# Attention with the two heads of a pair worked off side by side, in a two-layer hybrid encoder on one core

## The chip, the cores and the metric

The kernel runs on 1 core of one Trainium2 chip. The metric is the device time of one execution in microseconds (us); less is better. TensorE (PE; its weight loads stand apart as PEld), VectorE (DVE), ScalarE (ACT), GpSimd (POOL) and the DMA queues work side by side and wait for each other by semaphores.

## The reference, cut to what matters

One sequence of 512 tokens with 1024 features goes through two layers. Each layer has a mixer (a state-space part S5, six heads of latent attention MLA, six heads of forget-gate attention FOX, normalised, merged and projected back) and a feed-forward part: dense in the first layer, eight experts with two per token in the second. The attention that the change touches is a softmax over the keys up to the end of the queries' block of 128:

```
def block_sweep(q, k, v, scale, mask_fn, log_decay=None):
    for qb in range(L // Q_BLOCK):                 # 4 blocks of 128 queries
        q0, q1 = qb * Q_BLOCK, (qb + 1) * Q_BLOCK
        s = q[:, :, q0:q1] @ k[:, :, :q1]^T * scale
        if log_decay is not None:
            s = s + log_decay[:, :, q0:q1, None] - log_decay[:, :, None, :q1]
        s = where(mask, s, -inf)
        p = softmax(s)
        outs.append(p @ v[:, :, :q1])
    return concatenate(outs, axis=2)
```

A head is 64 wide in v. All of it is float32.

## The kernel before

Program order is written in Python; which instruction stands where in an engine's own queue is laid down before the run by a planner (`tile.TileContext(nc, schedule_with_timeline_sim=True)`), which plays the program through and takes, on each engine, the earliest in program order of what is ready. A tile's buffer is taken when its first writer is placed, and comes free with its last reader. On the chip each engine then works strictly through its queue.

**Layers.** `layer_mix` walks the strings of `SEQ` (L104, L105): a letter is a step, among them `f` and `m` (project and lay out a pair of heads of FOX or MLA), `s` and `o` (S5), `a` (adaLN vectors, each piece a DMA of 512 KB into one buffer and a product on DVE, L473 to L482; held behind the last pair of heads laid out, L471), `A` (attention of the next pair that was laid out), `g` (merge one mixer's output), `w` (one eighth of the output projection). There are six pairs of heads in a layer, three of FOX and three of MLA, so six `A` steps.

**A pair of heads.** `attend` (L893) goes through head 0's four query tiles and then head 1's, eight tiles in all. For tile i with n = i + 1 key blocks:

- `att_prob` (L860): the logits into a bank of PSUM group A (two banks; L867, and the mask at L868), the maximum on DVE (L871), the exponential with its sum on ACT into a tile `pr` of 128 x 512 (L872; `NPR` = 3 buffers), the reciprocal (L873) and the scaling by it (L874: on GpSimd for i = 0 and 2, on DVE for i = 1 and 3).
- `att_out` (L877), traced two tiles later (`ADP` = 2): n transposes of `pr` into a bank of PSUM group B (three banks; L883), one copy to the tile `PT` on ACT (L886; two buffers), and n products with v (L888), each 64 output rows wide. Head 0 puts out to rows 0 to 63 of the pair's bank `po`, head 1 to rows 64 to 127; `po` is one more bank of group B. A float32 product is two instructions on the PE queue.
- after the last tile `po` is copied to the pair's place in the mixer's output (L891).

**The output projection** `out` (L1235) borrows the buffers of `pr` for a tile `xs` of x: loaded by a DMA on ACT's queue (L1237), updated on DVE from PSUM (L1244), and stored by another DMA on ACT's queue (L1245). After the mixer x is loaded again from there (L1264) and the MLA part of the projection is added (L1272, L1273).

Of the kernel before, what the change touches and what calls it, by code (L numbers as in the profile page):

```python
# [10 lines left out]
FT = mybir.dt.float32  # L11
# [38 lines left out]
# places of all experts, and of all but the last two  # L50
# [3 lines left out]
def _most_blocks():  # L54
    """The most blocks of 128 tokens that can be left over, for any counts of the experts."""
# [3 lines left out]
    while todo:  # L59
        r, top, used, k = todo.pop()  # L60
        best = max(best, k)
        if r == NE or (r, top, used, k) in seen:
            continue
        seen.add((r, top, used, k))
        # the smallest counts at which rank r leaves j blocks, and the same count as the rank before
        for n in {min(top, CAP[r])} | {CAP[r] + P * j + 1 for j in range(NT)} | {top}:
            if n <= top and used + n <= 2 * L:
                todo.append((r + 1, n, used + n, k + max(0, -(-(n - CAP[r]) // P))))
# [14 lines left out]
NPR = 3  # L83
# [114 lines left out]
def lay(inputs):  # L198
# [11 lines left out]
    # the scales of the first norm with their inputs on partitions  # L210
# [76 lines left out]
class Net:  # L287
    def __init__(self, ctx, tc, a, out, dbg=None, depth=DEPTH, stop=None):
# [10 lines left out]
        # what needs other activation tables  # L299
# [18 lines left out]
    def consts(self):  # L318
# [11 lines left out]
        for l in range(DEPTH):  # L330
# [8 lines left out]
            # the gains of q and k meet in the products: k carries both  # L339
# [16 lines left out]
    def bank(self, side=None):  # L356
        """A bank of PSUM: of the group asked for, or of each in turn."""
# [9 lines left out]
    def wload(self, src, n, eng=None, pool=None, tag="", bufs=2):  # L367
        """A piece of a weight as two parts that the tensor engine takes in one pass each."""
# [18 lines left out]
    def exp_ln(self):  # L387
        """The activation tables with both Exp and Ln, for what is traced in the block this opens."""
# [8 lines left out]
    def mm3(self, ps, a, b, start, stop, shared=False):  # L397
        """Three passes; shared: the bank holds two groups, and the first start clears it for both."""
# [5 lines left out]
    def rsqrt_of(self, ps, n, m, out, tmp):  # L404
        """1 / sqrt(ps / n + EPS)"""
# [13 lines left out]
    def sigmoid(self, x, scale):  # L419
        """x = 1 / (1 + exp(-scale x)), the exponential kept finite."""  # L420
# [41 lines left out]
    def ada_prep(self):  # L462
        """silu(c), with its features on partitions and along the free dimension."""
# [5 lines left out]
    def held(self):  # L469
        """What VectorE gets in the block stays behind the last pair of heads laid out."""  # L470
# [16 lines left out]
    def norm_sum(self, x, groups):  # L487
        """The sum of squares of each token, on all partitions; the squares of a group are added up beforehand."""
# [12 lines left out]
    def norm_rms(self, ps, cut=1):  # L501
        """1 / the root mean square of each token, on all partitions, in parts that can be had one by one."""
# [9 lines left out]
    def norm_block(self, x, k, r, A, sh, h, s=slice(0, L)):  # L512
        """A block of features, normalised and modulated, in two parts."""
# [22 lines left out]
    def start(self, x, h, names, ps):  # L536
        """The first norm block by block, as the weights of its modulation come in, and what the blocks give to the
        first projections."""
# [57 lines left out]
    def angles(self, pool):  # L596
        """Sines and cosines of the positions and of what S5 turns by, in a step and in a chunk of 8; its decays."""
# [31 lines left out]
    def powers(self, t, tmp, last):  # L629
        """t[i, :, k] = t[i, :, 0] ** (k + 1), complex."""  # L630
# [8 lines left out]
    def s5_mats(self, l, q0, nq, pool):  # L639
        """The matrices of nq pairs of groups: inputs to states, states to outputs, inputs to outputs in a chunk."""  # L640
# [32 lines left out]
        # (lam_bar - 1) / lam  # L673
# [26 lines left out]
        # -Im(H) and Re(H): the conjugate of C and of the powers gives Re(H) and -Im(H)  # L700
# [13 lines left out]
        # the two groups of a pair side by side, each on its own half of the rows  # L714
# [25 lines left out]
        # the rotation of chunk j by 8 j times the angle, and the decay of a chunk  # L740
# [11 lines left out]
    def s5_part(self, l, u, c, yj, pool):  # L752
        """A quarter of the groups: the chunks' states by a scan, and what the groups put out."""
# [72 lines left out]
    def s5_out(self, l, yj, pool):  # L826
        """The gated output, features on partitions."""
# [15 lines left out]
        # gelu(y) = y sigmoid(2 sqrt(2 / pi) (y + 0.044715 y^3))  # L843
# [16 lines left out]
    def att_prob(self, un, hh, i, pool):  # L860
        """The softmax of a head for a tile of queries."""
# [8 lines left out]
        pr = pool.tile([P, L], FT, tag="pr", name="pr", bufs=NPR)  # L870
# [6 lines left out]
    def att_out(self, un, hh, i, pr, po, pool, oT):  # L877
        """Its product with v, by keys on partitions."""
        nc = self.nc
        ps = self.bank("B")  # L880
        n = (i + 1) * P
        for j in range(i + 1):
            nc.tensor.transpose(ps[:, j * P:(j + 1) * P], pr[:, j * P:(j + 1) * P], self.C("ident"))  # L883
        PT = pool.tile([P, L], FT, tag="PT", name="PT", bufs=NPT)
        eng = nc.scalar.copy if (hh * NT + i) % 8 in PTA else nc.vector.tensor_copy
        eng(PT[:, :n], ps[:, :n])  # L886
        for j in range(i + 1):
            nc.tensor.matmul(po[hh * 64:hh * 64 + 64, i * P:n], un["v"][:, j, un["vo"] + hh, :],  # L888
                             PT[:, j * P:(j + 1) * P], start=(j == 0), stop=(j == i))
        if hh == 1 and i == NT - 1:  # L890
            nc.scalar.copy(oT[:, un["u"], :], po)  # L891

    def attend(self, un, pool, oT):  # L893
        """A pair of heads: the softmax of a tile runs ahead of the product of the one before."""
        po = None
        for hh in range(2):
            for i in range(NT):
                pr = self.att_prob(un, hh, i, pool)
                self.att_end(ADP)
                if po is None:  # L900
                    po = self.bank("B")
# [1007 lines left out]
```

## Time and profile before

| | us |
|---|---|
| median of 3 runs | 1623.21 |
| lowest, highest of the 3 | 1614.22, 1625.42 |
| span of the profiled execution, first to last instruction | 1614.5 |

The profiled execution is thus like the fastest of the three runs. In the order of time the span holds the start and the first layer's mixer (to about 345 us), the dense feed-forward part (to about 740 us), the second layer's mixer (to about 1004 us) and the experts. Matmuls are pipelined and a matmul's length in the profile covers its way through the array, so the distance from start to start is what one costs in a row of them. Queue waits are inferred from semaphores.

### The profile page before, as it was taken

The page shows a single profiled execution, that of the slowest core. Times are in us where ns is not written, and L with a number is a line of the kernel's source. Part 1 is how long each engine was busy: PE and PEld are TensorE (multiplying, and loading weights), DVE is VectorE, ACT ScalarE, POOL GpSimd, SP SyncE. Part 2 cuts the span into 40 slices and gives each one's busy share as a digit, 9 for nine tenths or more (in the row PEclk, how much of TensorE's full clock was granted, in tenths as well). Part 3 has the DMA queues.
Part 4 walks back from the last instruction along what each step waited for, and adds up shares of the span by engine and source line. Part 5 has one row for each costly group of instructions (what it writes and reads, how often), then busy time and mean ns, then how long its engine had stood idle before and what let it go on. Part 6 is the DMA issues. An engine that isn't in the chain of part 4 may idle for free.

```text
span 1614.5 us, 25527 instructions
## 1 busy us (share of the span) xinstructions
PE 1524.0 (94%) x8907; PEld 1288.6 (80%) x8907; DVE 1129.4 (70%) x2628; ACT 805.2 (50%) x1547; POOL 200.7 (12%) x279
## 2 busy tenths in 40 slices
PE   6989999889999999999999999599999999999997
PEld 5877776568888788888877667489889999998995
DVE  7695677775855577556455565778678878877876
ACT  4344357443322232234345763366566766766762
POOL 1223131111000000003221120100000001003002
PEclk7988899989999999999999999789999999999998
DMA  9323341575566657553321006377688878878886
GB/s 358 132 91 124 118 134 46 189 274 158 182 200 187 228 168 233 174 169 115 115 78 48 1 8 221 114 247 270 233 275 298 281 236 309 304 260 297 305 281 212
DMA packets 94823, 309.62 MB, mean 192 GB/s; under 512 B 12065, under 2 KB 12513, under 8 KB 94689
## 3 DMA queue, kind: packets, MB, share of 16 engines
q1 hardware_dynamic: 74736, 252.89, 47.0%
q0 software_dynamic: 13040, 42.45, 7.7%
q10 hardware_dynamic: 6912, 12.59, 2.3%
q8 instruction: 72, 1.18, 0.3%
q14 instruction: 63, 0.51, 0.1%
HBM read 283.79 MB, written 24.10 MB: 191 GB/s over the span
## 4 chain that ended last, share of the span: by engine, by line
PE 66%; DMA 14%; DVE 11%; issue 4%; ACT 3%; POOL 1%; SPq 0%; DVEq 0%; ACTq 0%; POOLq 0%
DMA adw<-in_wada_dram 6%; PE psB L401 4%; PE psB L400 4%; PE psB L402 4%; PE psC L401 3%; PE psC L400 3%; PE psC L402 3%; PE psB L888 3%; PE psA L402 3%; PE psA L400 3%; PE psA L401 3%; PE psA L867 3%; PE psB L1427 2%; PE psA L1427 2%; DVE adw L478 2%
## 5 line engine op out<-in xcount | busy, mean ns | idle before, releaser
L383 ACT CAST wh<-wr 128x1024 fp32r<-128x1024 f32 (+4 forms) x402 | 396.8, 993 | 424.5 <-PE psB L401 90.4
L384 DVE TENSOR_TENSOR wl<-wr,wh 128x1024 fp32r<-128x1024 f32 (+4 forms) x402 | 459.1, 1149 | 162.8 <-ACT wh L383 158.2
L478 DVE SCALAR_TENSOR_TENSOR adw<-adw,cact 128x1024 f32<-128x1024 f32 x80 | 98.1, 1227 | 75.5 <-DMA adw<-in_wada_dram 75.4
L1427 PE MATMUL psB<-hgB,wh 128*128 128x480 f32 (+3 forms) x256 | 85.3, 341 | 0.0
L867 PE MATMUL psA<-U 65*128 65x128 f32 (+3 forms) x192 | 72.2, 463 | 8.3 <-DVE xn L981 7.6
L871 DVE TENSOR_REDUCE ms<-psA 128x1 f32<-128x128 f32 (+1 forms) x96 | 46.4, 485 | 45.6 <-PE psA L868 45.1
L1429 PE MATMUL psB<-hgB,wl 128*128 128x256 f32 x256 | 72.2, 282 | 0.0
L1427 PE MATMUL psC<-hgB,wh 128*128 128x480 f32 (+3 forms) x192 | 65.9, 348 | 0.2 <-ACT wh L383 0.2
L874 POOL TENSOR_SCALAR pr<-pr,ms 128x128 f32<-128x128 f32 (+1 forms) x48 | 49.0, 1021 | 136.5 <-DVE ms L873 100.2
L400 PE MATMUL psB<-fh,wh 128*128 128x512 f32 (+1 forms) x156 | 61.2, 392 | 4.7 <-ACT fh L518 4.7
L1427 PE MATMUL psA<-hgB,wh 128*128 128x480 f32 (+3 forms) x184 | 63.1, 350 | 1.0 <-ACT wh L383 0.7
L401 PE MATMUL psB<-fh,wh 128*128 128x512 f32 (+1 forms) x156 | 60.9, 390 | 0.3 <-DVE fh L523 0.3
L402 PE MATMUL psB<-fh,wl 128*128 128x512 f32 (+1 forms) x156 | 60.6, 388 | 0.0
L872 ACT ACTIVATE pr<-psA,ms 128x128 f32<-128x128 f32 (+1 forms) x96 | 51.4, 537 | 18.0 <-DVE ms L871 13.2
L1507 POOL DMA_DIRECT2D yd<-yt x21 | 11.8, 563 | 375.9 <-ACT yt L1497 263.1
L886 ACT COPY PT<-psB 128x128 f32<-128x128 f32 (+1 forms) x96 | 41.5, 435 | 31.5 <-PE psB L883 31.2
L1429 PE MATMUL psA<-hgB,wl 128*128 128x256 f32 x184 | 53.3, 290 | 3.0 <-DVE wl L384 3.0
L1429 PE MATMUL psC<-hgB,wl 128*128 128x256 f32 x192 | 55.2, 287 | 0.0
L1427 PEld LDWEIGHTS psB<-hgB,wh 128*128 128x128 f32 x256 | 48.4, 189 | 1.6
L1429 PEld LDWEIGHTS psB<-hgB,wl 128*128 128x128 f32 x256 | 48.4, 189 | 0.2
L867 PEld LDWEIGHTS psA<-U 65*128 65x128 f32 (+1 forms) x192 | 32.4, 204 | 14.9 <-issue 11.1
L883 PE MATMUL psB<-cst,pr 128*128 128x128 f32 x240 | 44.2, 290 | 0.0
(772 smaller groups left out, 4608.4 us busy)
## 6 DMA issues: line engine op xcount, KB each, us to landing
adw<-in_wada_dram SPq DMA_DIRECT2D x80, 512.0 KB, 3.8
wr<-in_md_dram SPq DMA_DIRECT2D x80, 512.0 KB, 4.5
wr<-in_mg_dram SPq DMA_DIRECT2D x79, 512.0 KB, 4.7
wr<-in_mu_dram SPq DMA_DIRECT2D x78, 512.0 KB, 4.7
wr<-in_fg_dram SPq DMA_DIRECT2D x22, 512.0 KB, 4.4
wr<-in_fu_dram SPq DMA_DIRECT2D x22, 512.0 KB, 4.4
wr<-in_me_dram SPq DMA_DIRECT2D x16, 512.0 KB, 4.3
wr<-in_w_f_dram SPq DMA_DIRECT2D x12, 512.0 KB, 3.7
```

The costliest lines, as they stand in the source:

```text
L383: nc.scalar.copy(hi[:, :n], raw[:, :n])
L384: nc.vector.tensor_tensor(out=lo[:, :n], in0=raw[:, :n], in1=hi[:, :n], op=OP.subtract)
L400: mm(ps, a[0], b[0], start=start, stop=False, skip_group_check=shared)
L401: mm(ps, a[0], b[1], start=False, stop=False, skip_group_check=shared)
L402: mm(ps, a[1], b[0], start=False, stop=stop, skip_group_check=shared)
L478: nc.vector.scalar_tensor_tensor(out=w, in0=w, scalar=1.0, in1=self.cact, op0=OP.mult, op1=OP.mult, accum_out=self.ada[l][:, j:j + 1])
L867: nc.tensor.matmul(ps[:, :n], U[0:r, 2 + hh, i * P:n], U[0:r, hh, 0:n], start=True, stop=False)
L872: nc.scalar.activation(pr[:, :n], ps[:, :n], AF.Exp, bias=ms[:, 0:1], accum_out=ms[:, 1:2])
L874: (nc.gpsimd if (hh * NT + i) % 8 in PRP else v).tensor_scalar(pr[:, :n], pr[:, :n], ms[:, 1:2], None, op0=OP.mult)
L888: nc.tensor.matmul(po[hh * 64:hh * 64 + 64, i * P:n], un["v"][:, j, un["vo"] + hh, :], PT[:, j * P:(j + 1) * P], start=(j == 0), stop=(j = ...
L1427: mm(ps[:, :2 * C], hi[:, s], h2, start=(kk == 0), stop=False, skip_group_check=True)
L1429: mm(ps[:, C:C + 2 * P], lo[:, s], h2[:, 0:2 * P], start=False, stop=(kk == KD - 1), skip_group_check=True)
```

## The change

All comments and docstrings are dropped, which moves line numbers and nothing else. What is computed stays the same.

- `attend` goes through the four tiles and takes both heads of a tile together; `att_out` gets both heads' probabilities, transposes and copies one head after the other, and then runs the products key block by key block, head 0 and head 1 in turn.
- What was traced two tiles later is now traced two pairs of tiles later.
- `pr` becomes two tiles by the parity of i, `pr0` of 384 columns and `pr1` of 512, with two buffers each in place of three of 512.
- `out` takes its `xs` from `pr1`, and so has two buffers in place of three.

```diff
-NPR = 3
+NPR = 2
 NPT = 2
@@ att_prob
-        pr = pool.tile([P, L], FT, tag="pr", name="pr", bufs=NPR)
+        pr = pool.tile([P, L - P + P * (i % 2)], FT, tag=f"pr{i % 2}", name="pr", bufs=NPR)
@@
-    def att_out(self, un, hh, i, pr, po, pool, oT):
-        """Its product with v, by keys on partitions."""
+    def att_out(self, un, i, prs, po, pool, oT):
         nc = self.nc
-        ps = self.bank("B")
         n = (i + 1) * P
+        PTs = []
+        for hh, pr in enumerate(prs):
+            ps = self.bank("B")
+            for j in range(i + 1):
+                nc.tensor.transpose(ps[:, j * P:(j + 1) * P], pr[:, j * P:(j + 1) * P], self.C("ident"))
+            PT = pool.tile([P, L], FT, tag="PT", name="PT", bufs=NPT)
+            eng = nc.scalar.copy if (hh * NT + i) % 8 in PTA else nc.vector.tensor_copy
+            eng(PT[:, :n], ps[:, :n])
+            PTs.append(PT)
         for j in range(i + 1):
-            nc.tensor.transpose(ps[:, j * P:(j + 1) * P], pr[:, j * P:(j + 1) * P], self.C("ident"))
-        PT = pool.tile([P, L], FT, tag="PT", name="PT", bufs=NPT)
-        eng = nc.scalar.copy if (hh * NT + i) % 8 in PTA else nc.vector.tensor_copy
-        eng(PT[:, :n], ps[:, :n])
-        for j in range(i + 1):
-            nc.tensor.matmul(po[hh * 64:hh * 64 + 64, i * P:n], un["v"][:, j, un["vo"] + hh, :],
-                             PT[:, j * P:(j + 1) * P], start=(j == 0), stop=(j == i))
-        if hh == 1 and i == NT - 1:
+            for hh, PT in enumerate(PTs):
+                nc.tensor.matmul(po[hh * 64:hh * 64 + 64, i * P:n], un["v"][:, j, un["vo"] + hh, :],
+                                 PT[:, j * P:(j + 1) * P], start=(j == 0), stop=(j == i))
+        if i == NT - 1:
             nc.scalar.copy(oT[:, un["u"], :], po)
 
     def attend(self, un, pool, oT):
         po = None
-        for hh in range(2):
-            for i in range(NT):
-                pr = self.att_prob(un, hh, i, pool)
-                self.att_end(ADP)
-                if po is None:
-                    po = self.bank("B")
-                self.pend.append(lambda hh=hh, i=i, pr=pr, po=po: self.att_out(un, hh, i, pr, po, pool, oT))
+        for i in range(NT):
+            prs = [self.att_prob(un, hh, i, pool) for hh in range(2)]
+            self.att_end(ADP)
+            if po is None:
+                po = self.bank("B")
+            self.pend.append(lambda i=i, prs=prs, po=po: self.att_out(un, i, prs, po, pool, oT))
@@ out
-                    xt = pool.tile([P, L], FT, tag="pr", name="xs", bufs=NPR)
+                    xt = pool.tile([P, L], FT, tag="pr1", name="xs", bufs=NPR)
```

## Rows read from the trace of the kernel before

**Rows 1.** The page, part 1: busy us, share of the span, instructions.

```profile
PE 1524.0 (94%) x8907; PEld 1288.6 (80%) x8907; DVE 1129.4 (70%) x2628; ACT 805.2 (50%) x1547; POOL 200.7 (12%) x279
```

**Rows 2.** Stretches: length, busy PE, PEld, DVE, ACT, POOL, then clock, DMA, GB/s.

```profile
100.00:262.00 162.00, 155.41 (x971) 119.02 (x970) 109.78 (x428) 81.69 (x233) 45.13 (x69) 0.91 0.34 108
262.00:345.00 83.00, 76.79 (x345) 53.45 (x344) 66.25 (x123) 46.40 (x92) 7.88 (x9) 0.98 0.61 211
831.00:982.00 151.00, 148.38 (x916) 106.26 (x915) 93.26 (x295) 97.23 (x256) 30.57 (x45) 1.00 0.12 37
```

**Rows 3.** Waits of PE in 831 to 982 us: total us, times, longest.

```profile
PE psB L888 <- ACT PT L886: 1.2, 3, 0.5
```

**Rows 4.** Timeline of PE at 216 us: start, length, line, tile, form, count.

```profile
215.77 0.50 PE L883 MATMUL psB<-cst,pr 128*128 128x128 f32 x3
216.19 0.65 PE L888 MATMUL psB<-PT,vm 128*64 128x128 f32 x4
216.77 0.66 PE L883 MATMUL psB<-cst,pr 128*128 128x128 f32 x4
217.27 0.60 PE L960 MATMUL psC<-cst,xn 128*65 128x128 f32 x4
217.70 0.60 PE L867 MATMUL psA<-U 65*128 65x256 f32 x2
```

**Rows 5.** Timeline of PE at 205 us, S5 and attention next to each other.

```profile
205.26 0.32 PE L822 MATMUL psD<-sB,sU 128*64 128x128 f32 x1
205.27 0.32 PE L888 MATMUL psB<-PT,vm 128*64 128x128 f32 x1
205.42 0.27 PE L822 MATMUL psD<-sB,sU 128*64 128x128 f32 x1
205.43 0.27 PE L888 MATMUL psB<-PT,vm 128*64 128x128 f32 x1
```

**Rows 6.** Timeline of PE at 858 us: S5's products, halves in turn.

```profile
858.14 0.69 PE L786 MATMUL psD<-sU,sC 128*64 128x64 f32 x16
858.66 0.60 PE L888 MATMUL psB<-PT,vf 128*64 128x128 f32 x4
```

**Rows 7.** Instructions of lines 888 and 886: ns min, median, max, first and last start.

```profile
L888 PE MATMUL psB<-PT,vf x240: 272/273/477, 121.0 to 934.5; 128*64 128x128 f32 x120
...
L886 ACT COPY PT<-psB x96: 252/460/672, 106.3 to 969.5; 128x128 f32<-128x128 f32 x24, 128x256 f32<-128x256 f32 x24, 128x384 f32<-128x384 f32 x24, 128x512 f32<-128x512 f32 x24
...
  PEld psB L888: 9.4, 17
```

**Rows 8.** Timelines of ACT and PE around two tiles' products at 950 us.

```profile
946.78 0.48 ACT L886 COPY PT<-psB 128x384 f32<-128x384 f32 x1
947.95 0.58 ACT L886 COPY PT<-psB 128x512 f32<-128x512 f32 x1 [0.22 <-PE psB L883]
...
950.21 0.87 PE L888 MATMUL psB<-PT,vm 128*64 128x128 f32 x6
```

**Rows 9.** Line 874, the scaling on GpSimd: ns min, median, max.

```profile
L874 POOL TENSOR_SCALAR pr<-pr,ms x48: 594/1233/2137, 103.1 to 962.4; 128x128 f32<-128x128 f32 x24, 128x384 f32<-128x384 f32 x24
```

**Rows 10.** Landing of the xs loads (L1237), then of the xs stores (L1245).

```profile
DMA to landing us min/median/max: 2.6/4.9/7.8
...
DMA to landing us min/median/max: 2.0/4.6/9.0
```

**Rows 11.** Line 1244 in 970 to 1004 us, six of its eight.

```profile
L1244 DVE SCALAR_TENSOR_TENSOR xs<-psC,ada,xs x6: 740/748/751, 976.4 to 1002.2; 128x512 f32<-128x512 f32 x6
```

**Rows 12.** The chain that ended last, 989 to 1003 us: start, us, what.

```profile
989.72 6.29 DMA xs<-xs
...
996.09 6.05 DMA xs<-xd
...
1003.02 0.38 PE psC L1537
```

**Rows 13.** The adaLN pieces of the first mixer: the chain, then line 478.

```profile
294.05 5.96 DMA adw<-in_wada_dram
...
L478 DVE SCALAR_TENSOR_TENSOR adw<-adw,cact x15: 1212/1224/1573, 226.5 to 349.3; 128x1024 f32<-128x1024 f32 x15
```

## The prediction

> **What bounds the kernel now.** I read the page first, for who is busy over the span: the tensor engine 94% of it [rows 1]. That share is an average, so next came the table by stretches. In the second layer's attention, 831 to 982 us, PE is busy 148.4 of 151.0 us while DVE has 93 and ACT 97: PE is the bound there [rows 2]. In the first layer, 100 to 262 us, it is 155.4 of 162.0, nearly the same but with more holes. From 262 to 345 us it is 76.8 of 83.0 [rows 2], and there the chain of waits runs through adaLN pieces: a load of up to 6.0 us into the one buffer, 1.2 us of DVE, the next load [rows 13]. So work taken from PE shortens the second layer's attention nearly one to one, the first layer's in part, and what stands behind its adaLN chain hardly at all. Then I read the timelines of PE, for what a product with v costs in its surroundings, and the views of the xs tiles, because the change takes one of their buffers.
>
> **The products side by side.** A pair of heads has 2 x (1+2+3+4) = 20 products of two instructions, 40; twelve pairs make the 480 of line 888, in two rows of 240 of which one is shown [rows 7]. In a row each costs what any 128-column float32 instruction does: the four of L960 take 217.70 - 217.27 = 0.43 us, 0.108 each [rows 4]. What two of them cost on different halves of the output rows the trace of before shows by chance: S5's last product and head 0's first stand next to each other, start 0.01 us apart, and so do their second instructions [rows 5]. That two halves in turn keep this up inside one bank is seen at S5's input products: sixteen 64-column instructions in 858.66 - 858.14 = 0.52 us, 0.033 each, where half of 0.108 would be 0.054 [rows 6]; that interval holds a change of form too. The queue takes instructions in order and each half can run one at a time. With a1 a2 b1 b2 a1 a2 ... the second of one head runs beside the first of the other, so 4n instructions of a pair of tiles need 2n + 1 places in time instead of 4n. Over n = 1 to 4 that is 24 places for 40: 16 saved, 16 x 0.108 = 1.73 us a pair, 10.4 us a layer.
>
> **The changes of form.** Between instructions with 64 and with 128 columns of the array PE loses time. Three transposes before a burst of products take 0.42 us to its start (0.095 over 3 x 0.108), the four products 0.58 us (0.15 over), the four transposes behind them 0.50 us (0.07 over) [rows 4]: 0.31 us a burst. There are at most 96 bursts, one for each copy to PT [rows 7]; both heads in one burst leave 48. That is 24 x 0.31 = 7.4 us a layer. The Trainium skill says the same in TensorEngine Tiling (Array Packing), Key Properties: changing the tiling mode drains the engine. It gives no price; the 0.31 us above is the trace's.
>
> **How much of it comes.** All of it is 17.8 us a layer, if both PT are there when PE reaches the products. None of it comes if the planner places head 0's products as soon as its PT is ready, while head 1's copy (0.25 to 0.67 us) still runs [rows 7]: head 0's block of at most eight instructions, 0.87 us, would be mostly gone by then. In before PE mostly comes late: a weight load of L888 waited for a PT only 17 times for 96 copies [rows 7], in the second layer PE waited 3 times, 1.2 us in all [rows 3], and at 950 us the next tile's PT had been finished (947.95 + 0.58) before the products of the tile ahead began [rows 8]. So about 80 of 100 are ready. The planner sees its own times and not the chip's, so I take 0.7: 12.4 us of PE time a layer.
>
> **The softmax in pairs.** Instructions, engines and sizes stay the same. New is that the exponential of tile i + 2 needs the buffer of tile i of the same parity, so it waits for the transposes of tile i; and for i = 0 and 2 both heads' scalings go to GpSimd one behind the other, 2 x 1.23 us [rows 9]. That loop (exponential, scaling twice, transposes 0.43 a head, copies) is some 5 us for two tiles' worth of both heads, against 151 / 6 / 2 = 12.6 us of PE work for them, so it is covered by the projections and logits that PE does meanwhile. Without that cover, in the last pair, it shows: 2 to 4 us a layer. Below it can cost nothing, above all of one GpSimd pair exposed twice in each pair of heads, 6 x 2 x 1.23 = 15 us a layer. It is nearer to the lower end, since PE waits so little today; I take 3 us in the second layer and 2 us in the first. The second bank of group B that both heads' transposes want is there (three banks, one for `po`), so at nothing; if a projection holds it, it is one copy late, 0.5 us.
>
> **The xs tiles.** Each of eight steps loads (median 4.9 us), updates (0.75), stores (4.6) [rows 10, 11], 10.3 us around one buffer and about 10.8 with issue. With three buffers the eighth step needs two rounds behind the first, with two it needs three: 32 us. The steps of the second layer spread over about 26 us today, up to 1002.2 [rows 11], and their end already waits: store 6.3 us, load 6.1 us, and only then PE's next [rows 12]. Behind the waiting update stand the release of its bank of group C and what DVE has queued; behind the store's wait on ACT's queue stand the casts of the next weights. So the last update comes 6 us later than it could. Least: nothing (three rounds at the shortest landings, 2.6 + 2.0 + 0.75, are 16 us). Most: at 7.8 and 9.0 us, 53 us against 26. PE has the MLA part of the projection to do meanwhile, so I take 4 us in the second layer and, with the slower transfers of 262 to 345 us but a longer spread, 3 us in the first.
>
> **The sum.** Second layer: -12.4 + 3 + 4 = -5.4 us. First layer: five of its six pairs lie ahead of 268 us, -10.3 us on PE; with holes and S5's loads on the path I count six tenths, -6; +2 and +3 behind: about -1 (what shortens the last pair goes into the wait for adaLN, which ends at 349.3 + 1.2 us [rows 13] and moves with the start of its pieces). Other stages do the same work. Together about -6.5 us: 1614.5 - 6.5 = 1608 us against the profiled execution. That one is like the fastest of three runs; the median, 1623.2, stands 8.7 us above it. Taken from the median: 1617 us.
>
> **Rivals.**
>
> *All of it comes, the tails stay hidden.* 17.8 us in the second layer and most of it, 11 to 15, in the first: 1623 - 30 = 1593 us. For it: PE busy 98% in the second layer [rows 2], and the two places where halves run together [rows 5, 6]. Against it: the planner, two buffers for xs.
>
> *The products don't run side by side.* A rule of the Trainium skill speaks for this: TensorE: Matmul & The Clock Gate, Part 3, "What overlaps and what doesn't", says that a weight load overlaps running matmuls only when the row group differs, and here both heads use all 128 rows. The trace disagrees: both products at 205 us hold 128 rows and still start together [rows 5], and the sixteen at 858 us too are on 128 rows [rows 6]. As a mechanism here, without overlap: only the changes of form are saved, 0.7 x 7.4 = 5.2 us a layer, less the new waits of 12 us: 1623 - 10 + 12 = 1625 us. The same time comes when the planner undoes the alternation.
>
> *Two xs buffers become the bound at both mixers' ends: slower.* At three rounds of 6.3 + 6.1 + 0.75 + 0.5 = 13.7 us [rows 12] the eight steps take 41 us against 26: +15 us in the second layer, about +10 in the first, where DMA is busy 0.61 [rows 2]; with 12 us gained on the way, 1623 + 25 - 12 = 1636 us. It decides when a round is over 1.5 times what PE needs for two steps. For it: that chain is on the path today. Against it: the first layer's spread is long already, and PE has other work.
>
> **How the numbers follow.** About 1% is what a measurement of this kernel can tell from no change, some 16 us; the three runs alone spread over 11. Forecast (1608 to 1624) 0.42; all of it (1588 to 1607) 0.27; no overlap or no alternation (1620 to 1632) 0.16; the xs bound (1630 to 1650) 0.15. Faster by over 1% is below 1607: the second case and a little of the first and third, whose ends reach there with the noise, 0.32. Slower by over 1% is above 1639: most of the last and a little for a planner that lays out queues worse elsewhere, 0.16. Within 1% is left with 0.52. The range leaves out the better end of the second and the worse end of the last: 1592 to 1637; the forecast's own is 1608 to 1624.
>
> **What would show it.** Right: products of the two heads starting in twos less than 0.02 us apart, in about 48 bursts; the second mixer's attention some 10 us shorter with PE still over 95% busy; the last update of xs 4 to 6 us later behind the last product with v than today. Wrong on the overlap: twos that start 0.108 us apart. Wrong on the alternation: runs of one head's products ahead of the other's. Wrong on the softmax: PE waits for `pr` or PT of more than 3 us a layer. Wrong on xs: eight updates within 26 us, or over 35. What would upset all of it is a change in length of the feed-forward or expert stages, of which no row here tells.

## The result and the profile after

The changed kernel takes 1637.8 us (median of four runs, 1633.4 to 1639.7) against 1622.0 us of the kernel before (four runs on the same chip, 1614.2 to 1625.4): ratio 1.0103, with a 95% interval of 1.008 to 1.0126. It is slower by about 1%, and it lies just outside the range forecast, 1592 to 1637 us (the forecast itself was 1617). The span of the profiled execution grew from 1614.5 to 1636.8 us.

The page's first part, as in [rows 1]: the engines did the same work, with PE busy 3.4 us less, in a longer span.

```profile
PE 1520.6 (93%) x8907; PEld 1278.6 (78%) x8907; DVE 1128.8 (69%) x2628; ACT 806.4 (49%) x1547; POOL 199.4 (12%) x279
```

The table by stretches (length, busy PE, PEld, DVE, ACT, POOL, granted clock, DMA share, GB/s). The first three lines answer [rows 2]; the second layer's attention starts 12 us later here, so its stretch is 843 to 994 us. The other three are stretches at the lower clock, which are read further down.

```profile
100.00:262.00 162.00, 155.92 (x1013) 116.70 (x1011) 113.02 (x437) 88.19 (x246) 45.95 (x70) 0.92 0.33 107
262.00:345.00 83.00, 69.78 (x297) 47.85 (x294) 61.76 (x112) 39.25 (x76) 5.71 (x8) 0.92 0.62 209
843.00:994.00 151.00, 143.29 (x904) 99.24 (x903) 92.15 (x291) 96.67 (x253) 28.33 (x44) 0.97 0.11 33
...
892.00:903.00 11.00, 10.07 (x40) 6.66 (x40) 3.21 (x14) 2.36 (x7) 1.63 (x6) 0.53 0.09 28
1022.00:1036.00 14.00, 12.08 (x35) 9.51 (x36) 7.18 (x12) 4.07 (x8) 1.59 (x3) 0.51 0.31 94
356.00:374.00 18.00, 10.23 (x32) 7.20 (x33) 13.37 (x25) 8.11 (x14) 4.24 (x2) 0.53 0.11 32
```

From 100 to 262 us PE got through 1013 instructions where it was 971: the first layer's attention did become quicker. From 262 to 345 us it is 297 for 345, and in the second layer's attention 904 for 916, at a clock of 0.97 for 1.00. So the loss begins where the last pair of layer 1 ends, and the second layer's attention gained nothing. To see where, I read four moments of each trace: the last product with v of a layer, the first block of layer 1's feed-forward norm, the first block of layer 2's first norm, the first product of the experts. All times are us.

| | before | after | difference |
|---|---|---|---|
| last product with v, layer 1 | 298.7 | 300.0 | +1.3 |
| from there to the feed-forward norm | 56.3 | 63.6 | +7.3 |
| to layer 2's first norm | 384.5 | 386.0 | +1.5 |
| to the last product with v, layer 2 | 233.3 | 236.0 | +2.7 |
| to the experts' first product | 80.1 | 87.9 | +7.8 |
| to the end | 561.5 | 563.3 | +1.8 |

Both tails behind attention, where the xs tiles work, lost 7 to 8 us. The attention itself, from which 12.4 us of PE time a layer should have come, lost a little as well.

**The products do run in twos.** The timeline of PE at 947 us (start, length, line, tile, form, count):

```profile
947.21 0.43 PE L893 MATMUL psB<-PT,vf 128*64 128x128 f32 x2
947.57 0.33 PE L886 MATMUL psB<-cst,pr 128*128 128x128 f32 x1
947.83 1.09 PE L893 MATMUL psB<-PT,vf 128*64 128x128 f32 x14
948.85 0.33 PE L886 MATMUL psB<-cst,pr 128*128 128x128 f32 x1
```

Fourteen instructions take 948.85 - 947.83 = 1.02 us to the next start. In a row of one head, at 0.108 each [rows 4], they would take 1.51. Counted over the trace, 155 of the 480 start within 0.03 us of the one before, where it was 2; a strict turn of the heads would give 240. The same lines show what went another way: head 0's first product (two instructions) stands alone ahead of the last transposes, before 947.83. PE changes form for it and back. There are 92 bursts of products in the trace, where it was 94.

**A new stall in the second layer.** The waits of PE (total us, times, longest), first in 843 to 994 us, where the second line answers [rows 3], then in 300 to 375 us, behind layer 1's attention:

```profile
PE psD L820 <- issue: 4.1, 1, 4.1
PE psB L893 <- ACT PT L889: 2.3, 4, 0.6
...
PE psA L498 <- ACT sq L493: 5.2, 1, 5.2
...
PE psB L400 <- ACT wh L383: 2.2, 1, 2.2
```

The timelines of PE and DVE around the first of these:

```profile
870.75 0.45 PE L786 MATMUL psD<-sU,sC 128*64 128x64 f32 x6
...
886.92 0.34 PE L786 MATMUL psD<-sU,sC 128*64 128x64 f32 x4
...
887.30 0.29 DVE L795 TENSOR_TENSOR sT<-sE,psD 128x128 f32<-128x128 f32 x1 [2.86 <-PE psD L786]
...
891.77 0.29 DVE L811 TENSOR_TENSOR sX<-sT 128x126 f32<-128x126 f32 x1
...
892.16 0.47 PE L820 MATMUL psD<-sA,sX 64*64 64x128 f32 x2 [4.10 <-issue]
```

S5's input products of one group were sixteen in a row in [rows 6]. In the new order of PE's queue the planner put them in four pieces over 16 us, and the last four instructions start at 886.92 us. Only then can DVE's chain begin, lines 795 to 811, at 887.30; S5's next product on PE waits for it and starts at 892.16. In the kernel before the group ended near 858.8, and its first user started at 878.5. Behind the 4.1 us of standing still the granted clock is at its lower level, 1.2 GHz, for 10.2 us: that is the stretch of 892 to 903 us above, at 0.53.

**The tails.** Line 1248 in 985 to 1020 us as in [rows 11], then who waited for the loads of line 1241, and their landing as in [rows 10]:

```profile
L1248 DVE SCALAR_TENSOR_TENSOR xs<-psC,ada,xs x6: 741/750/751, 988.6 to 1017.8; 128x512 f32<-128x512 f32 x6
...
L1241 ACTq DMA_DIRECT2D xs<-xd x8: 326/326/327, 979.5 to 1013.6; - x8
...
  DVE xs L1248: 10.3, 5
...
DMA to landing us min/median/max: 2.7/4.2/6.5
```

In the kernel before, updates waited for these loads 5.4 us, three times; now 10.3, five times, with landings that are no slower. Most of it lies in layer 1: there it is 7.2 us where it was 1.3, while in layer 2 it is 3.1 where it was 4.1. Line 1248 in 290 to 350 us with its wait for loads, then line 1244 of the kernel before in 290 to 340 us:

```profile
L1248 DVE SCALAR_TENSOR_TENSOR xs<-psC,ada,xs x6: 742/748/751, 299.1 to 332.5; 128x512 f32<-128x512 f32 x6
L1248 DVE SCALAR_TENSOR_TENSOR xs<-psD,ada,xs x1: 744/744/744, 346.8 to 346.8; 128x512 f32<-128x512 f32 x1
...
  DMA xs<-in_xT_dram: 7.2, 2
...
L1244 DVE SCALAR_TENSOR_TENSOR xs<-psC,ada,xs x6: 742/746/752, 305.9 to 333.5; 128x512 f32<-128x512 f32 x6
...
L1244 DVE SCALAR_TENSOR_TENSOR xs<-psD,ada,xs x1: 740/740/740, 336.7 to 336.7; 128x512 f32<-128x512 f32 x1
```

From first to last, the eight updates of layer 1 thus take 346.8 - 299.1 = 47.7 us, where it was 336.7 - 305.9 = 30.8. Those of layer 2 take 29.9 (the first, at 987.9, is not in the row shown), where it was 26.5. In layer 2 the chain that ended last (start, us, what), as in [rows 12]:

```profile
998.91 3.25 DMA xs<-xs
...
1002.18 5.96 DMA xs<-xd
...
1009.42 4.15 DMA xs<-xs
...
1013.64 0.33 ACTq L1241
...
1014.06 4.38 DMA xs<-xs
...
1018.83 3.55 DMA xs<-xs
```

Store, load, store, issue of the next load: from 998.9 to 1018.4 us the path is these transfers nearly alone. From 1022.1 us on the clock is at its lower level for 13.7 us, the stretch of 1022 to 1036 us above (3.4 us at this place in the kernel before). ACT issues loads and stores and also makes the weights' casts and the norm's squares; in layer 1's tail PE then stands for 5.2 and 2.2 us for those (second pair of the waits above), where the kernel before had waits of 1.3 us at most for ACT there, but for the 3.9 us at the start of the feed-forward that both have. From the longer of the two on the clock is at its lower level for 17.0 us, within the stretch of 356 to 374 us above, at 0.53 (10.2 us in the kernel before).

### The profile page after: what moved, and what is told of

Same layout as the page of the kernel before. It is cut to its first block, busy times and chain, and to the rows that moved or that the text cites. A ratio compares the mean times of both kernels' runs of the same rounds, so it can differ in the third digit from the quotient of the medians.

```text
span 1636.8 us, 25476 instructions
## 1 busy us (share of the span) xinstructions
PE 1520.6 (93%) x8907; PEld 1278.6 (78%) x8907; DVE 1128.8 (69%) x2628; ACT 806.4 (49%) x1547; POOL 199.4 (12%) x279
## 4 chain that ended last, share of the span: by engine, by line
PE 65%; DMA 15%; DVE 12%; issue 3%; ACT 3%; POOL 1%; ACTq 0%; DVEq 0%; SPq 0%; POOLq 0%
DMA adw<-in_wada_dram 6%; PE psB L401 4%; PE psB L400 4%; PE psB L402 4%; PE psC L400 4%; PE psC L401 4%; PE psC L402 4%; PE psA L401 3%; PE psA L402 3%; PE psA L400 3%; PE psA L867 3%; PE psB L893 2%; PE psB L1431 2%; DVE adw L478 2%; PE psB L886 2%
## 5 line engine op out<-in xcount | busy, mean ns | idle before, releaser
L867 PE MATMUL psA<-U 65*128 65x128 f32 (+7 forms) x192 | 71.4, 465 | 9.7 <-DVE xn L985 7.6
L871 DVE TENSOR_REDUCE ms<-psA 128x1 f32<-128x128 f32 (+3 forms) x96 | 46.1, 485 | 42.6 <-PE psA L868 39.0
L872 ACT ACTIVATE pr<-psA,ms 128x128 f32<-128x128 f32 (+3 forms) x96 | 51.0, 535 | 24.8 <-DVE ms L871 14.4
L889 ACT COPY PT<-psB 128x128 f32<-128x128 f32 (+3 forms) x96 | 40.1, 432 | 21.2 <-PE psB L886 15.7
L867 PEld LDWEIGHTS psA<-U 65*128 65x128 f32 (+1 forms) x192 | 32.2, 202 | 18.2 <-issue 12.4
```

The source lines that it names most:

```text
L867: nc.tensor.matmul(ps[:, :n], U[0:r, 2 + hh, i * P:n], U[0:r, hh, 0:n], start=True, stop=False)
L871: v.reduce_max(out=ms[:, 0:1], in_=ps[:, :n], axis=AX.X, negate=True)
L872: nc.scalar.activation(pr[:, :n], ps[:, :n], AF.Exp, bias=ms[:, 0:1], accum_out=ms[:, 1:2])
```

## The experiments

The change has three parts that can be had apart: the pair (both heads' tiles side by side), the turn of their products, and one xs place less. All kernels below compute the whole result. Ratios are against the kernel before, with 95% intervals.

| kernel | median us | ratio | interval |
|---|---|---|---|
| b_x2: before, two places for xs | 1639.1 | 1.0123 | 1.0067 to 1.018 |
| b_x3: before, every third xs tile in PT's buffers | 1619.5 | 1.0003 | 0.997 to 1.0035 |
| b_x5: before, every second xs tile in PT's buffers | 1623.3 | 1.0023 | 1.0002 to 1.0044 |
| after | 1637.8 | 1.0103 | 1.008 to 1.0126 |
| a_x3: after, three places | 1614.6 | 0.998 | 0.9959 to 1.0002 |
| a_noalt: after, heads one behind the other | 1653.3 | 1.0231 | 1.0179 to 1.0282 |
| a_noalt_x3: that, three places | 1642.1 | 1.0136 | 1.0089 to 1.0184 |
| a_full: after, strict turn | 1617.7 | 1.0001 | 0.9971 to 1.0032 |
| a_full_x3: that, three places | 1601.9 | 0.99 | 0.9864 to 0.9936 |
| a_x3_hp: a_x3, S5's products first | 1606.7 | 0.9919 | 0.9889 to 0.9948 |
| a_noalt_x3_hp: a_noalt_x3, S5's products first | 1630.7 | 1.0083 | 1.0055 to 1.0111 |
| a_full_x3_hp: a_full_x3, S5's products first | 1604.0 | 0.9893 | 0.9863 to 0.9923 |
| a_full_x4_hp: that, four places | 1603.1 | 0.9886 | 0.9857 to 0.9915 |

**Two places for xs, and nothing else.** In the kernel before, the xs tiles use PT's two buffers.

```
-                    xt = pool.tile([P, L], FT, tag="pr", name="xs", bufs=NPR)
+                    xt = pool.tile([P, L], FT, tag="PT", name="xs", bufs=NPT)
```

> The kernel before, with one edit: the output projection's xs tile takes its buffers from PT (two) in place of pr (three). Theory xs (two buffers set the end of both mixers): about 8 us later at each mixer's end, 12 to 18 us slower in all, ratio 1.007 to 1.011; the last xs update of the second mixer 3 to 8 us later behind the last product with v than before's 29.3 us. Rival planner (the time of the changed kernel comes from where the planner places S5's and the heads' products): the attention is as before here, so under 4 us, ratio 0.998 to 1.0025.

Measured 1.0123, some 20 us, a little above the range expected: that alone is as much as the whole change lost. Line 1244 in 970 to 1030 us, and who waited for the loads of line 1237:

```profile
L1244 DVE SCALAR_TENSOR_TENSOR xs<-psC,ada,xs x6: 739/748/752, 990.7 to 1022.5; 128x512 f32<-128x512 f32 x6
...
  DVE xs L1244: 8.1, 4
```

The eight updates take 1022.5 - 990.1 = 32.4 us instead of 26.5 (in layer 1, 44.9 instead of 30.8), and the tail behind the last product with v takes 68.6 us in layer 1 (56.3 before) and 85.6 in layer 2 (80.1).

**A third place in the changed kernel.** Every third xs tile uses PT's buffers.

```
-                    xt = pool.tile([P, L], FT, tag="pr1", name="xs", bufs=NPR)
+                    xt = pool.tile([P, L], FT, tag="PT" if d % 3 == 2 else "pr1", name="xs", bufs=2)
```

> The changed kernel, with one edit: every third xs tile takes its buffer from PT, so there are three places for xs again. Theory xs: both tails come back, 12 to 18 us faster than the changed kernel, ratio to before 0.999 to 1.003. Rival planner: the tails are not what was lost, ratio to before stays at 1.008 to 1.012.

Measured 0.998: 1.0103 - 0.998 = 0.0123, 20 us, come back, the same figure from the other side. Line 1248 in 965 to 1005 us, the loads and who waited for them:

```profile
L1248 DVE SCALAR_TENSOR_TENSOR xs<-psC,ada,xs x6: 742/746/751, 974.2 to 998.6; 128x512 f32<-128x512 f32 x6
...
L1241 ACTq DMA_DIRECT2D xs<-xd x8: 326/336/418, 965.1 to 992.6; - x8
...
  DVE xs L1248: 1.0, 2
```

The updates wait 1.0 us for loads instead of 10.3, those of layer 1 take 27.8 us instead of 47.7, and the tails are 49.4 and 76.7 us (63.6 and 87.9 with two places). PE's wait of 5.2 us for ACT's squares is gone, and the one of 2.2 us for its casts is 0.2. But this kernel, too, only draws level with the kernel before: its 155 products in twos have won nothing that is left.

**The owner of the buffer.** The same exchange of every third buffer in the kernel before.

```
-                    xt = pool.tile([P, L], FT, tag="pr", name="xs", bufs=NPR)
+                    xt = pool.tile([P, L], FT, tag="PT" if d % 3 == 2 else "pr", name="xs", bufs=NPT if d % 3 == 2 else NPR)
```

> Kernel before, three places for x's slices as before, every third one in PT's buffers in place of pr's: the control for the exchange of buffers by itself. Theory: the number of places counts, not whose they are, 1616 to 1622 us, ratio 0.998 to 1.002. Rival, that the buffers' owner matters (PT's are freed later): over 1.004.

Measured 1.0003. pr has three buffers and serves two tiles of three here, so a buffer comes round after four or five steps and not after three as the expectation says: it is a control with rather more places. Neither that nor PT's buffers make a difference. With two places the loss is the same in PT's buffers (b_x2) and in pr1's (after): the number of places did it, not whose they are.

**No turn.** The products of head 0, then those of head 1, in the changed kernel.

```
-        for j in range(i + 1):
-            for hh, PT in enumerate(PTs):
+        for hh, PT in enumerate(PTs):
+            for j in range(i + 1):
```

> The changed kernel, with the products of head 0 ahead of all of head 1's: pairs of tiles, buffers and the rest as in the changed kernel, no alternation. Theory overlap: the 155 second-of-twos of the changed kernel cost 0.108 us each again, 16.8 us of PE time, so 8 to 15 us slower than the changed kernel, ratio to before 1.015 to 1.02. Rival (the attention is not bound by PE any more, the placing of S5's products decides): within 5 us of the changed kernel or faster, ratio 1.005 to 1.013; here the planner keeps S5's input products together, in 8 groups for 10.

Measured 1.0231, above the first theory's range: the turn is worth 1.0231 - 1.0103 = 0.0128, 21 us. The timeline of PE at 940 us shows what an untouched row costs:

```profile
939.97 1.09 PE L893 MATMUL psB<-PT,vm 128*64 128x128 f32 x8
940.99 0.33 PE L886 MATMUL psB<-cst,pr 128*128 128x128 f32 x1
```

Eight instructions take 1.02 us here, as long as fourteen did above. Overlap on two halves of the array's columns is real and it is the turn that brings it.

**The pair by itself.** The same with three places, so that only the pair is left of the change.

> Changed kernel with three places for x's slices, and head 0's products all ahead of head 1's: the pairs and their softmax without any alternation. If alternation and places add up: 14 to 16 us above the 1614.6 us with alternation, so 1628 to 1632 us, ratio 1.005 to 1.009: the pair by itself, without twos, then loses against the kernel before. If the pair alone costs nothing (the prediction's sum for the pair, without overlap and without fewer changes of form): 1617 to 1622 us, ratio 0.999 to 1.003.

Measured 1.0136, above both sides of the expectation: the pair by itself costs 22 us. With the turn 0.0136 - (-0.002) = 0.0156, 25 us, come back, and the loss of a place takes 20. Along this path of runs the three add up to the result, as they must: +22 - 25 + 20 = +17 us, 1.0103. The pair holds the two `pr` tiles and the longer deferral as well; no run takes these apart. The two longest waits of PE in layer 1's attention, 120 to 315 us, that the kernel before doesn't have:

```profile
PE psD L853 <- DVE yT L848: 3.6, 1, 3.6
PE psC L964 <- DVE kq L1048: 2.7, 1, 2.7
```

With the turn (a_x3) the first is gone; the second is there and longer, 4.5 us. The pair's other place is the second layer's S5 stall: 4.2 us at line 820, and the lower clock for 13.7 us behind it. Here the input products are in one piece, but the planner set them at 894.3 us, right ahead of their use at 900.0.

**S5's input products first.** In the kernel with three places, a higher priority in the planner for the eight products of line 786.

```
+        with self.tc.high_priority():
             for i in range(2):
                 for q in range(nq):
...
```

> Changed kernel with three places for x's slices, and S5's eight input products (L786) traced at a higher priority, so that the last group of layer 2 is not split by products of the attention. Theory that the 4.1 us stall and the clock at half behind it (13.7 us in the kernel with three places alone) are a cost of their own: the stall is gone and 6 to 11 us come off 1614.6: 1603 to 1609 us, ratio 0.990 to 0.994. Rival, that the stall only takes time that the next wait for PSUM banks would have taken: 1612 to 1617 us, ratio 0.996 to 1.000.

Measured 0.9919, 8 us below 1614.6 (10 by the ratios), in the middle of the first theory. PE's order up to that group is the same. The timeline of PE, and the table by stretches from the first product with v of layer 2 on:

```profile
863.14 0.69 PE L787 MATMUL psD<-sU,sC 128*64 128x64 f32 x16
```

```profile
835.00:986.00 151.00, 149.04 (x940) 103.50 (x939) 101.78 (x306) 99.41 (x258) 29.54 (x46) 1.00 0.15 49
```

The sixteen are in one piece at 863 us, the stall and the lower clock behind it are gone, and PE does 940 instructions in 151 us where it did 916 in [rows 2]. From layer 2's first norm to the last product with v it is 226.6 us (236.4 in a_x3, 233.3 before). That is 6.7 of the 9.4 us (12.4 less 3) that the prediction had expected of this layer's attention, and one stall had eaten them. The whole gain rests on the medians: the two profiled executions are level, 1611.4 us for 1610.3, since in this one, the slowest of its seven, the last product with v of layer 1 comes 7.7 us later (307.7 for 300.0) although the order on PE is the same up to there.

**The same for the pair by itself.**

> The pair without alternation, three places for x's slices, S5's input products at higher priority: their last group of layer 2, which stood right ahead of its use (last product 894.8 us, use 900.0 us), then stands 91 instructions earlier. If S5's late group is a part of what the pair costs by itself, as it was with alternation (8 us), 1632 to 1636 us, ratio 1.007 to 1.011, and some 15 us of the pair's cost are left to the waits of layer 1 for DVE (kq 2.7 us, yT 3.6 us, with the clock at half behind them). If the group is all of it, 1618 to 1624 us, ratio under 1.003. If PE would have waited elsewhere, no change: 1640 to 1644 us, ratio 1.012 to 1.015.

Measured 1.0083, as the first theory has it: 1.0136 - 1.0083 = 0.0053, 8.6 us, of the pair's 22 are S5's late group; the two intervals overlap. The other 13 lie in layer 1: its last product with v is at 316.2 us (298.7 before), while from there to the experts each stretch is within 4 us of the kernel before. The two waits for DVE of 3.6 and 2.7 us are still in that trace, with the lower clock behind them for 13.7 and 6.8 us. What delays DVE's kq and yT there wasn't taken away in a run, so that these waits are the 13 us is argued and not shown; and as a_x3 has a wait for kq of 4.5 us with its last product at 300.0 us, that wait is not enough by itself.

**A strict turn.** Head 1's first product goes ahead, and all others are issued behind it.

```
+        first = prod(1, 0)
+        with self.tc.issue_after(first.ins):
+            for j in range(i + 1):
+                prod(0, j)
+                if j < i:
+                    prod(1, j + 1)
```

> The changed kernel, with the products of a pair of tiles in strict turn, head 1's first at the front and all others held behind it on the tensor engine's queue, so that none is placed before both PT are copied; about 51 bursts of products in place of 88. Theory planner (head 0's first product alone ahead keeps the number of changes of form as it was): 40 bursts fewer at about 0.3 us are 11 us of PE time, and some 2 us more of overlap; where attention is bound by PE, 6 to 11 us faster than the changed kernel, ratio to before 1.003 to 1.007. Rival softmax (the wait for both heads costs as much as it gives): PE waits for PT grow by over 5 us and the ratio stays at 1.009 to 1.013.

Measured 1.0001, 16 us below the changed kernel, more than expected. There are 51 bursts and 240 products in twos. The timeline of PE at 939 us:

```profile
938.90 1.09 PE L892 MATMUL psB<-PT,vf 128*64 128x128 f32 x16 [0.20 <-ACT PT L889]
939.92 0.33 PE L886 MATMUL psB<-cst,pr 128*128 128x128 f32 x1
```

Sixteen instructions in 1.02 us. This order also happens to leave S5's group in nearly one piece, so the 4 us stall of layer 2 is gone with it; the tails are as long as in the changed kernel (63.5 and 85.2 us).

**Strict turn and three places.**

> Changed kernel with both repairs: the output projection's slices of x get three places again (every third one in PT's buffers), and head 1's first product goes ahead with all the others issued after it, so that all pairs alternate strictly. If the two costs are separate, the roughly 20 us that two places cost comes off the 1617.7 us of the strictly alternating kernel: 1594 to 1603 us, ratio 0.986 to 0.991, about 51 bursts, 240 products that start within 0.03 us of the one before, last update of x's slices in layer 2 by about 987 us. If the strict turn had already won back part of what the slices lost (it delays the tail's other work), 1605 to 1615 us, ratio 0.993 to 0.998.

Measured 0.99, 0.9864 to 0.9936: faster than both kernels, by the expected sum. **With S5's products first, and with a fourth place:**

> Strict turn, three places for x's slices, and S5's input products at higher priority. In the kernel with the first two alone the last group of these products lay within 1.8 us (859.2 to 861.0 us) and no stall of S5's chain was left in layer 2, so if the priority helps only by removing that stall, nothing comes off 1601.9 us: 1597 to 1605 us, ratio 0.987 to 0.992. Rival, that the priority moves other work for the better as well and its gain of 8 us in the kernel without strict turn was not the stall: 1592 to 1596 us, ratio 0.983 to 0.986.

> The same with four places for x's slices (two of pr1's buffers and two of PT's in turn). Theory that with three places the tail is bound by TensorE's products and no longer by the loads of the slices (in layer 2, 25.7 us from first to last update with three places, 26.5 in the kernel before, 29.9 with two): under 3 us come off, 1597 to 1605 us, ratio 0.986 to 0.992, the eight updates of layer 2 still 23 us or more apart. Rival, that each place counts: another 8 to 20 us, 1582 to 1594 us, ratio under 0.985.

Measured 0.9893 and 0.9886. These three can't be told apart. The priority adds nothing where the stall was gone already, and a fourth place adds nothing, although the eight updates of layer 2 come closer, 963.5 to 986.3 us, 22.8. **More places in the kernel before,** every second tile in PT's buffers, a buffer free again after four to six steps:

> Kernel before with five places for x's slices (three of pr's buffers, two of PT's in turn). Same question on the side of the kernel before: 2 places gave 1639, 3 gave 1619. If three are enough: 1615 to 1620 us, ratio 0.997 to 1.001. If each place counts: under 1612 us, ratio under 0.996.

Measured 1.0023, a little above the first range and far from the second. From three places on, another one is worth nothing; from two to three it is 15 to 20 us (0.0095 to 0.0123 in the four kernels that were run with both).

## Why the prediction was wrong

**The products side by side: right.** 16 of 40 places a pair were to fall away, 192 in all. 155 did, 0.81 of these where 0.7 was taken. (In strict turn it is 240, 20 of 40: two first instructions start together and not, as the step had it, the second of one head beside the first of the other, so that 4n instructions need 2n places.) In layer 2, from each start of a product with v to the next one's, the sum over PE's timeline is 23.2 us before and 14.6 after, 8.6 us less, for 10.4 x 0.7 = 7.3 forecast. The time shows more than that. The sum's 18.4 us (12.4 and 6) hold the changes of form too; of it the twos are 7.3 in layer 2 and by the same steps some 3.7 in layer 1, 11 together, and the turn brought 25. On PE's timeline, from a_noalt_x3 to a_x3, the same sum of starts falls from 22.5 to 14.7 us in layer 2 and from 21.7 to 15.1 in layer 1, 14.4 together. The other 11 of the 25 us lie in what else differs between the two orders that the planner laid out, which no run takes apart. The rival without overlap is out: a_noalt, which has 19 twos, is what it would look like. As the prediction said at [rows 5, 6], products on two halves of the columns that both hold all 128 rows start together. The Trainium skill's rule for weight loads (TensorE: Matmul & The Clock Gate, Part 3, "What overlaps and what doesn't") lets them overlap running products only in another row group, which the rival took as no overlap here; the runs decide against that. In the changed kernel's trace the weight loads do so too: one of 948.00 to 948.13 us lies, by the profile, inside a product of 947.99 to 948.27, both on 128 rows.

**The changes of form: wrong.** 48 bursts were forecast and 92 came, so of the 0.7 x 7.4 = 5.2 us a layer nothing came. The step took the 0.7 from how often both PT are ready when PE arrives. It should have asked what the planner does with the one product that it sees ready first: it sets it alone, and the rest in turn. With the strict turn, the starts into and out of the bursts of layer 2 sum up to 12.4 us for 26 bursts (a_full_x3) where it is 21.3 for 45 in the changed kernel, 8.9 us less, 0.47 a burst; the forecast's price of 0.31 us would make it 19 x 0.31 = 5.9. The Trainium skill names a drain at a change of tiling (TensorEngine Tiling (Array Packing), Key Properties); the 0.47 us a burst is what went with it here. In the time it shows less: with the stall gone, the strict turn is worth 0.9919 - 0.9893 = 0.0026, 4 us with overlapping intervals. From layer 2's first norm to the last product with v it saves 226.6 - 221.9 = 4.7 us, and the tail behind is 4.5 us longer (82.8 for 78.3).

**The softmax in pairs: the first term that failed.** It was put at +5 us and cost 22. The waits that the step priced, for pr and PT, stayed small: 2.3 us in layer 2, and in layer 1 4.5 (1.1 for PT, 3.4 until the exponential into pr frees a bank), a little over the 3 us that the prediction named as its sign. What it left out is that the planner's whole order moves with the pair: S5's products were split or put late (8 us of stall and lower clock, by the two kernels with S5's products first), and in layer 1 DVE's work for the next pair is late (the other 13, as far as the traces tell). That the order moves because twice as many instructions become ready at once is an explanation that no run tests. The sentence on "a planner that lays out queues worse elsewhere" stood only beside the chances, with no price.

**The xs tiles: the second term that failed, and the one that decides.** The mechanism was right: a round of load, update and store through two places. The size was not: +7 in the sum, 15 to 20 in the runs. In layer 2 the spread was forecast near 32 us and measured 29.9 (26.5 before). The step that failed most is layer 1: it was put at 3 us, since the spread there is long already, and that spread grew from 30.8 to 47.7 us, beyond the 35 that the prediction gave as a sign of being wrong. All four kernels with two places have 44.9 to 47.7 us there, all with more have 25.6 to 32.6. The prediction had named what stands behind the wait, the bank of group C and the casts on ACT's queue, and then set PE's other work against it. That cover was not there: in layer 1 PE waits next for ACT's casts and squares, which it doesn't with three places, and the pauses have the lower clock behind them. Between 120 us and the first expert product the clock is at its lower level for 102 us after and for 67 before, 76 in a_x3 and 87 in b_x2; but it is 91 in a_noalt and 99 in a_noalt_x3, so it does not follow the places alone, and how much of the 20 us is the clock's is not shown. Layer 1, priced lower, lost more: its tail is 14 us longer with two places than with three, layer 2's 11 (25 in the two profiled executions, 20 by the ratios).

**The rivals.** The third came, at 1636 us, for other reasons than it gave. It had the eight steps of layer 2 at 41 us, a loss of 25 and a gain of 12 on the way; measured are 29.9 (47.7 in layer 1), 20, and 3. Its total was right by luck, because two errors cancelled: the loss at the places is smaller and the pair eats the gain.

**The sum in the runs' numbers:** -25 for the turn (forecast -18), +22 for the pair (+5), +20 for the places (+7): +17 us where -6 was forecast. The 25 and the 22 depend on the order in which the parts are taken. What does not: pair and turn together brought 3 us (a_x3, with an interval that reaches 1.0002) where 13 were forecast, and of the 10 us that are missing the S5 stall took 8 to 10; the places cost 13 us more than forecast.

## What to carry to other kernels

Count the places that a change takes from a tile's pool against the round trip of what goes through them, and then follow what is queued behind the wait, up to the clock: here one buffer of three cost 15 to 20 us, most of the 25 that the turn brought, and a fourth was worth nothing. Look at each place where the tile is used: the loss was largest where the prediction had taken the spread as long already. When a change makes more instructions ready together, look at where the planner puts the long chains of other parts (here S5's products, whose DVE chain needs 5 us of other PE work to hide), and fix their order if need be. An alternation that is only written in the loop is not an alternation in the queue: order it behind the instruction that becomes ready last.

## What the runs showed of the hardware

Products on two halves of the array's columns, on the same 128 rows and into one bank, run two at a time for as long as they take turns: sixteen instructions in 1.02 us, as long as eight of one half. A stall of PE of 4.1 us had the lower clock behind it for 10.2 us (after) and 13.7 us (a_x3), and taking the stall away (a_x3_hp) brought 8 us by the medians, twice its length; that the lower clock is the other half fits these stretches and was not run by itself.
